# A branch moved into an earlier stage, and identity products in four of TensorE's waits, in a hybrid decoder layer

## The chip, the core and the metric

The kernel runs on one core of one Trainium2 chip. The metric is the device time of one execution in microseconds. The profile names the engines of the core: PE is TensorE's matmul, PEld its weight load, DVE is VectorE, ACT is ScalarE, POOL is GpSimd, and SP is SyncE, whose queue issues most of the transfers.

## The reference

One layer of a decoder for a prompt of 1024 tokens and a sample of 8 sequences with 4 new tokens each, over a paged cache of 8192 positions. A normalised input is projected once and feeds two groups of heads: A, attention over the 256 keys that a small indexer picks for each query, and B, a retention in chunks of 128. All is float32.

```python
h = _rmsnorm(x, g_pre)
qa, ka, va, qi, ki, wi, ga, qb, kb, vb, gb = _project(h, w_in, pos)
# A: indexer, top 256, softmax over the picked keys with a relative bias
s = einsum('bqhd,bsd->bqhs', qi, ki) * D_IDX ** -0.5
score = einsum('bqh,bqhs->bqs', wi, relu(s))        # masked to kpos <= qpos
idx = top_k(score, 256)
oa = softmax(qa . ka[idx] * HEAD_DIM ** -0.5 + rel_bias[bucket]) . va[idx]
# B: per chunk of 128
inter = (qc * dec_in) . S
intra = ((qc . kc) * dmat) . vc
S = S * dec_chunk + (kc * dec_out) . vc
# merge
y = concat(silu(ga) * oa, silu(gb) * head_norm(ob)) . w_out
x = x + _rmsnorm(y, g_post)
x = x + (p . w_ple_up) * sigmoid(x . w_ple_gate)
```

## The kernel before, in words

The kernel is written with a tile framework: the program says which operation an engine does on which tile, a scheduler with a timeline of its own orders each engine's instructions, roughly by their place in the program and by when their operands should be ready, and each engine then works through its queue in that order. What is emitted earlier is preferred. A branch (`tc.If`) divides the program: what stands behind it is put into no queue ahead of what stands before it. `tc.issue_after(x)` keeps the instructions of its block behind `x` in their engine's queue, without a wait.

A float32 product is done either as three products of rounded halves (high and low parts, lines 255 to 257 and 265 to 267), or as one float32 product, which the trace shows as two instructions. PSUM is dealt out in banks of 512 columns through `bank(name, tag)`, with a fixed number of buffers for each tag.

The stages in the order of the program:

1. **First blocks.** Blocks of 128 tokens are loaded, normalised (`norm_x`, line 530 on DVE), transposed on PE and split into high and low parts (`transpose_split`, lines 221, 226 and 227). The norm of three blocks is emitted first; then the first projections follow (`proj_b`), with the rest of the blocks between.
2. **Index scores of the prompt.** For six blocks of 128 queries (`index_scores`, lines 353, 354, 496 and 500). Each block's scores go to `score`.
3. **The sample's index stage.** A loop of 8 sequences by 2 halves, 16 passes. Each pass gathers a piece of the key cache (`kx`, line 797), transposes it on PE (`ptx`, line 807), copies it on ACT (`kT`), multiplies (`pox`, line 811) and applies relu on ACT (`rl`). `later()` emits what was put off: `head_sum` and `by_key`, whose `xe` copies are on DVE (line 786). `unit(1.4)` emits pieces of the projections of `qa`, `ka`, `va` and `ga`. And `tickb` drives the generator `bp`, the prompt's bisection.
4. **The prompt's bisection** (`bisect_prompt`) finds the 256th largest score of each row. It counts (line 659 on DVE, line 655 on ACT for the two longest rows) and fixes one bit per step, then looks at the low half (lines 692 and 694), and takes the eight largest (`top`, line 700). If the tie at the threshold needs more than eight of them, a slow path is taken: `anywhere` sums a flag over the partitions on PE (`pfl`, line 624), DVE reads it (`flp`, line 626) and a branch on DVE (line 709) skips the slow path or not. Behind the branch the masks are made, one block of queries per step (lines 727 to 734).
5. **Retention**, four pairs of heads (`hp`). For each of 8 token blocks PE projects q and k (`pqk`), DVE does the rotary step (`rope`, `rp`, lines 1034 to 1036, finished on POOL); then for each of 8 blocks PE projects v and gate (`pvg`) and `chunk_mm` and what follows do the chunk (lines 1055 to 1065, 1456, 1461 on DVE, 1465, 1467). After the last block `ret_sample` does the sample (lines 1113 to 1135, with `dst` in line 1129). `steps(hp)` is called at each block: it drives the sample's bisection `bss` (`su`, `jv`, `sjk`, `stot`) in the first pair and the sample's selection later, and in the first pair two steps of `bp`. `norm_gate` ends a pair.
6. **Attention of the prompt**, 8 blocks of queries by 2 key heads by 4 heads: scores (`sa`, lines 1563 and 1564), bias and minimum on DVE (line 1569), exponential on ACT (line 1572), transposes (`ptp`, line 1579), products with v (`ob`, line 1587). The sample's attention runs in between.
7. **Merge**: output projection, norm, gate and up projections.

Of the kernel before, what the change touches and what calls it, by code (L numbers as in the profile page):

```python
# [22 lines left out]
NS = 32  # L23
# [97 lines left out]
def tile_step(ctx: ExitStack, tc: tile.TileContext, I, O):  # L121
    nc = tc.nc
# [28 lines left out]

    cst = cp.tile([128, CW], F32, name="cst")

    def C(name, rows=128):
        o, w = _CW[name]
        return cst[:rows, o:o + w]

    ident = C("ident")
# [55 lines left out]
    xl = xp.tile([128, KC, T + NS], F32R, name="xl")  # L214
    xs = xp.tile([128, KC, NS], F32, name="xs")

    def transpose_split(dst_h, dst_l, dst, src, rows):

        pt = pair("pt")
        for c in range(8):  # L220
            nc.tensor.transpose(pt[:, c * rows:(c + 1) * rows], src[:rows, c * 128:(c + 1) * 128],
                                ident[:rows, :rows])
        pt = pt[:, :8 * rows].rearrange("p (j r) -> p j r", j=8)
        for a in range(2):
            ks = slice(a * 4, a * 4 + 4)
            nc.scalar.copy(dst_h(ks), pt[:, ks])
            nc.vector.tensor_tensor(dst_l(ks), pt[:, ks], dst_h(ks).bitcast(F32), op=ALU.subtract)
            if dst is not None:
                nc.vector.tensor_copy(dst[:, ks], pt[:, ks])
# [146 lines left out]
    tickb = [0.0]  # L376
# [89 lines left out]
    with pool("ix", side="right") as ix:  # L466
# [99 lines left out]
            xin[i] = load_x(i)  # L566
        for i in range(3):
            norm_x(i)
        wt.append(load_w("qi1", wcols((QI + 256, 256))))
        nc.sync.dma_start(cst[:, 128:], I["const"][:, 128:CW])  # L570
        todo = list(range(3, 9))
# [221 lines left out]
    for b in range(8):  # L793
        rls = []
        for a in range(2):
            kx = sx.tile([128, 2048], F32, tag="kx", bufs=2, name="kx")
            nc.gpsimd.indirect_dma_start(
                out=kx, out_offset=None, in_=pages,
                in_offset=bass.IndirectOffsetOnAxis(ap=kidx[:, a * 8 + b:a * 8 + b + 1], axis=0))
            for up in range(2):  # L800
                pt = pair("ptx")
                kT = sx.tile([128, 1024], F32, tag="kT", bufs=2, name="kT")
                for u2 in range(2):
                    for i in range(4):
                        r2 = up * 8 + i * 2 + u2
                        c0 = u2 * 512 + i * 128
                        nc.tensor.transpose(pt[:, c0:c0 + 128], kx[:, r2 * 128:(r2 + 1) * 128], ident)
                nc.scalar.copy(kT, pt)
                po = bank("pox", "t")
                for u2 in range(2):  # L810
                    nc.tensor.matmul(po[u2 * 64:u2 * 64 + 64, :], qbd[:, b, :], kT[:, u2 * 512:u2 * 512 + 512],
                                     start=True, stop=True)
                rl = sx.tile([128, 512], F32, tag="rl", bufs=6, name="rl")
                nc.scalar.activation(rl, po, AF.Relu)
                rls.append(rl)
            later()
            tickb[0] += 1.5
            while tickb[0] >= 1:
                tickb[0] -= 1
                step(bp)  # L820
            unit(1.4)
        pend.append(lambda b=b, rls=rls: head_sum(b, rls))
# [219 lines left out]
    def take_vg(src, rows, tb, hp, name):  # L1042
# [6 lines left out]
        nc.scalar.activation(sg[:rows], src[:rows, 128:256], AF.Silu)  # L1049
        return vv.rearrange("p h v -> p (h v)"), sg  # L1050

    def chunk_mm(qk, vv, tb, rows, mask_ap, hp):

        r = bank("ret", "c")
# [7 lines left out]
        sm = rt.tile([128, 2, 128], F32, tag="sm", bufs=2, name="sm")  # L1062
        for j, sc in enumerate((r[:rows, 256:256 + rows], e[:rows, :rows])):
            js = slice(j * 64, j * 64 + 64)
            nc.tensor.matmul(sc, qkT[js, 128:128 + rows], qkT[js, 0:rows], start=True, stop=True)
            nc.vector.tensor_tensor(sm[:rows, j, :rows], sc, mask_ap, op=ALU.mult)
        return r, qkT, sm

# [37 lines left out]
    def ret_sample(hp, qk, sh, acc):  # L1106
# [8 lines left out]
            o = r[NS * (b % 4):NS * (b % 4) + NS, 0:128]  # L1115
            nc.tensor.matmul(o, qm[:, b, :], s0[:, b, :], start=(b < 4), stop=(b >= 4 and b % 4 > 1))
        for j in range(2):
            nc.tensor.matmul(r[NS * j:NS * j + NS, j * 64:j * 64 + 64], sm[:NS, j, :NS], vv[:NS, j * 64:j * 64 + 64],
                             start=False, stop=True)
        nc.scalar.copy(acc[:NS, 8, :], r[NS:2 * NS, 0:128])  # L1120
        for j in (0, 2, 3):
            nc.vector.tensor_tensor(acc[:NS, 8, :], r[NS * j:NS * j + NS, 0:128], acc[:NS, 8, :], op=ALU.add)
# [1 line left out]
        for j in range(2):  # L1124
# [1 line left out]
            vm = rt.tile([NS, 8, 64], F32, tag="vm", bufs=1, name="vm")  # L1126
            nc.vector.tensor_tensor(vm, vv[:NS, None, js].to_broadcast([NS, 8, 64]),
                                    bmask[:, :, None].to_broadcast([NS, 8, 64]), op=ALU.mult)
            nc.tensor.matmul(d[js], qk[:NS, 128 + j * 64:192 + j * 64], vm, start=True, stop=True)
        so = rt.tile([128, 8, 64], F32, tag="vm", bufs=1, name="sso")  # L1130
        for j in range(2):
            js = slice(j * 64, j * 64 + 64)
# [289 lines left out]
    for hp in range(4):  # L1422
# [24 lines left out]
        for tb in range(8):  # L1447
# [10 lines left out]
            for j in range(2):  # L1458
# [3 lines left out]
                else:  # L1462
                    nc.vector.tensor_copy(nxt[js, js], o[js, js])
            if tb:
                nc.tensor.matmul(o, qkT[:, :128], sbd[tb % 2], start=True, stop=False)
            for j in range(2):
                nc.tensor.matmul(o[:, j * 64:j * 64 + 64], sm[:, j, :], vv[:, j * 64:j * 64 + 64],
# [68 lines left out]
    for qb in range(8):  # L1536
# [11 lines left out]
        for kv in range(2):  # L1548
# [5 lines left out]
            for i4 in range(4):  # L1554
                h = 4 * kv + 2 * (i4 % 2) + i4 // 2
                L = (atl, at)[kv].tile([128, T], F32, tag="L", bufs=4, name="L")
                P.append(L)
                mn = ap_.tile([128, 4], F32, tag="mn", bufs=4, name="mn")
                least, i = 3.0e38, 0
                for c in range(0, n, 512):  # L1560
                    wc = min(512, n - c)
                    s = bank("sa")
                    nc.tensor.matmul(s[:, :wc], qas[:, h, :], kah[kv][:, c:c + wc], start=True, stop=False)  # L1563
                    nc.tensor.matmul(s[:, :wc], qas[:, h, :], kal[kv][:, c:c + wc], start=False, stop=True)  # L1564
                    cut = min(max(n - w, c), c + wc)
                    for x0, x1, add in ((c, cut, mask[:, OFF.get(qb, 0) + c:OFF.get(qb, 0) + cut]),
                                        (cut, c + wc, near[:, h - 4 * kv, cut - n + 256:c + wc - n + 256])):
# [243 lines left out]
```

## Time and profile before

| what | value |
|---|---|
| median of 3 runs | 1076.75 us (1073.38 to 1078.46) |
| the profiled execution's own time | 1065.73 us |
| its span, first to last instruction | 1063.9 us |
| mean granted TensorE clock | 0.973 |
| PE busy | 991.7 us, 93% of the span |
| DVE, ACT, POOL busy | 66%, 47%, 27% |
| HBM read and written | 79.25 MB and 21.68 MB |

The page counts for each engine how long it was busy. A row of a timeline reads: start, duration in us, engine, line and operation, what it writes from what, and in square brackets how long the engine was idle before and what ended that wait. A row of the waits reads: who waited for whom, us in total, how often, the longest. The granted clock is 1.00 at full speed of TensorE and 0.50 at half.

### The profile page before, as it was taken

The page shows a single profiled execution, that of the slowest core. Times are in us where ns is not written, and L with a number is a line of the kernel's source. Part 1 is how long each engine was busy: PE and PEld are TensorE (multiplying, and loading weights), DVE is VectorE, ACT ScalarE, POOL GpSimd, SP SyncE. Part 2 cuts the span into 40 slices and gives each one's busy share as a digit, 9 for nine tenths or more (in the row PEclk, how much of TensorE's full clock was granted, in tenths as well). Part 3 has the DMA queues.
Part 4 walks back from the last instruction along what each step waited for, and adds up shares of the span by engine and source line. Part 5 has one row for each costly group of instructions (what it writes and reads, how often), then busy time and mean ns, then how long its engine had stood idle before and what let it go on. Part 6 is the DMA issues. An engine that isn't in the chain of part 4 may idle for free.

```text
span 1063.9 us, 19686 instructions
## 1 busy us (share of the span) xinstructions
PE 991.7 (93%) x7375; PEld 838.6 (79%) x7375; DVE 699.8 (66%) x2012; ACT 504.2 (47%) x1092; POOL 288.1 (27%) x287
## 2 busy tenths in 40 slices
PE   3899998998999789999989995999999999999998
PEld 2899997676776778898788893666656899989998
DVE  6847768999401798978986957887764424874332
ACT  5445554986434356842333435656544523442211
POOL 3102223111201532423632512634340521222100
PEclk8999999999999989999989996899999999999999
DMA  8211235546343311112201425623211312432211
GB/s 291 65 60 51 79 96 169 186 145 202 126 164 111 70 40 41 37 48 87 61 24 41 119 86 149 190 79 105 75 56 47 117 41 80 148 111 82 86 37 40
DMA packets 98308, 102.24 MB, mean 96 GB/s; under 512 B 21346, under 2 KB 88386, under 8 KB 95906
## 3 DMA queue, kind: packets, MB, share of 16 engines
q1 hardware_dynamic: 92450, 74.74, 23.3%
q0 software_dynamic: 5760, 26.22, 7.9%
q8 instruction: 58, 0.95, 0.4%
q14 instruction: 40, 0.33, 0.1%
HBM read 79.25 MB, written 21.68 MB: 95 GB/s over the span
## 4 chain that ended last, share of the span: by engine, by line
PE 53%; DVE 8%; ACT 2%; DMA 2%; issue 1%; POOL 1%; SPq 0%; DVEq 0%; ACTq 0%; POOLq 0%
PE ob L1587 4%; PE ptp L1579 4%; PE pg L265 3%; PE pg L267 3%; PE pg L266 3%; PE po L265 3%; PE po L266 2%; PE po L267 2%; PE pvg L265 2%; PE pvg L266 2%; PE pvg L267 2%; PE sa L1563 2%; PE sa L1564 2%; PE pqk L265 2%; PE pqk L266 1%; PE pqk L267 1%
## 5 line engine op out<-in xcount | busy, mean ns | idle before, releaser
L1147 POOL DMA_INDIRECT kvs<-in_cache_kv,idx x64 | 63.6, 994 | 84.1 <-ACT pT L1584 44.7
L265 PE MATMUL pqk<-whi_qkb,xh 128*128 128x256 f32 x256 | 74.5, 291 | 5.5 <-DVE rp L1036 5.5
L265 PE MATMUL pvg<-whi_vgb,xh 128*128 128x256 f32 x256 | 77.4, 302 | 1.6 <-DVE need L729 1.5
L266 PE MATMUL pvg<-wlo_vgb,xh 128*128 128x256 f32 x256 | 76.6, 299 | 0.0
L267 PE MATMUL pvg<-whi_vgb,xl 128*128 128x256 f32 x256 | 75.2, 294 | 0.0
L266 PE MATMUL pqk<-wlo_qkb,xh 128*128 128x256 f32 x256 | 73.5, 287 | 0.0
L265 PE MATMUL po<-whi_o,yTh 128*128 128x256 f32 x256 | 73.1, 286 | 0.4 <-DVE yaT L1598 0.4
L267 PE MATMUL pqk<-whi_qkb,xl 128*128 128x256 f32 x256 | 73.0, 285 | 0.0
L267 PE MATMUL po<-whi_o,yTl 128*128 128x256 f32 x256 | 72.8, 285 | 0.0
L265 PE MATMUL pg<-whi_g,yTh 128*128 128x256 f32 x256 | 72.7, 284 | 0.0
L266 PE MATMUL po<-wlo_o,yTh 128*128 128x256 f32 x256 | 72.7, 284 | 0.0
L267 PE MATMUL pg<-whi_g,yTl 128*128 128x256 f32 x256 | 72.3, 282 | 0.0
L266 PE MATMUL pg<-wlo_g,yTh 128*128 128x256 f32 x256 | 72.2, 282 | 0.0
L500 DVE SCALAR_TENSOR_TENSOR score<-r,wi,score 128x384 f32<-128x384 f32 (+5 forms) x42 | 44.2, 1053 | 21.0 <-ACT r L496 19.9
L1572 ACT ACTIVATE L<-L,mn 128x128 f32<-128x128 f32 (+7 forms) x64 | 49.5, 775 | 13.7 <-DVE mn L1569 13.6
L265 PEld LDWEIGHTS pqk<-whi_qkb,xh 128*128 128x128 f32 x256 | 48.2, 188 | 9.6 <-issue 6.8
L1768 DVE TENSOR_TENSOR sgm<-pu,sgm 128x256 f32<-128x256 f32 x32 | 13.5, 423 | 61.8 <-PE pu L267 58.6
L265 PEld LDWEIGHTS pvg<-whi_vgb,xh 128*128 128x128 f32 x256 | 50.6, 197 | 3.7 <-issue 1.7
L266 PEld LDWEIGHTS pvg<-wlo_vgb,xh 128*128 128x128 f32 x256 | 50.7, 198 | 0.5
L267 PEld LDWEIGHTS pvg<-whi_vgb,xl 128*128 128x128 f32 x256 | 50.6, 198 | 0.6
L265 PEld LDWEIGHTS po<-whi_o,yTh 128*128 128x128 f32 x256 | 49.0, 191 | 2.2 <-issue 1.6
L496 ACT ACTIVATE r<-si 128x384 f32<-128x384 f32 (+5 forms) x48 | 36.3, 758 | 30.3 <-PE si L354 29.0
(540 smaller groups left out, 3262.1 us busy)
## 6 DMA issues: line engine op xcount, KB each, us to landing
wraw_qkb<-in_w_in SPq DMA_DIRECT2D x16, 256.0 KB
wraw_vgb<-in_w_in SPq DMA_DIRECT2D x16, 256.0 KB
wraw_o<-in_w_out SPq DMA_DIRECT2D x8, 512.0 KB
qas<-qas_d SPq DMA_DIRECT2D x8, 512.0 KB
xr<-in_x_prompt SPq DMA_DIRECT2D x8, 512.0 KB
wraw_g<-in_w_ple_gate SPq DMA_DIRECT2D x8, 512.0 KB
out_y_prompt<-sgm SPq DMA_DIRECT2D x32, 128.0 KB
qas_d<-qst SPq DMA_DIRECT2D x8, 384.0 KB
```

Source lines behind the costliest of these rows:

```text
L265: nc.tensor.matmul(pt[:, :n], ah, hi[:, k, :n], start=(k == 0), stop=False)
L266: nc.tensor.matmul(pt[:, :n], ah, lo[:, k, :n], start=False, stop=False)
L267: nc.tensor.matmul(pt[:, :n], al, hi[:, k, :n], start=False, stop=(k == kc - 1))
L496: nc.scalar.activation(r[:, :n], s[:, :n], AF.Relu)
L500: nc.vector.scalar_tensor_tensor(sc, r[:, :n], wi[:, qb, h:h + 1], sc, op0=ALU.mult, op1=ALU.add)
L1147: return nc.gpsimd.indirect_dma_start(out=dst, out_offset=None, in_=kvflat, in_offset=bass.IndirectOffsetOnAxis(ap=idx, axis=0))
L1563: nc.tensor.matmul(s[:, :wc], qas[:, h, :], kah[kv][:, c:c + wc], start=True, stop=False)
L1564: nc.tensor.matmul(s[:, :wc], qas[:, h, :], kal[kv][:, c:c + wc], start=False, stop=True)
L1572: behind[0] = nc.scalar.activation(L[:, :n], L[:, :n], AF.Exp, bias=least, scale=-1.0, accum_out=sm[:, i4:i4 + 1])
L1579: nc.tensor.transpose(tp[:, i4 * 128:i4 * 128 + 128], P[i4][:, kb * 128:kb * 128 + 128], ident)
L1587: nc.tensor.matmul(ob[64 * o:64 * o + 64, :256], vtok[:, kb, kv * 64:kv * 64 + 64], pT[:, o * 256:o * 256 + 256], start=(kb == 0), stop=(k ...
L1768: nc.vector.tensor_tensor(sg[:rows], usrc, sg[:rows], op=ALU.mult)
```

## The change

It has two parts.

The first is one number. In the sample's index stage `tickb` grows by 2.5 instead of 1.5 per pass, so up to 40 instead of 24 steps of `bp` are emitted in its 16 passes. `bp` has 31 steps.

The second is a helper, `hold(n, behind, tag, w)`: it takes a PSUM bank and emits `n` float32 products of the identity with `w` columns of the table of constants, one behind another, the first of them behind the instruction `behind`. Their result is not read. It is called in four places:

- 40 products of 128 columns behind the last transpose of the second block, ahead of the third block's norm;
- 3 products of 512 columns behind the scores of the last block of the last pair in the retention, ahead of line 1465's product;
- in the last pair's `ret_sample`, 2 and 3 products of 512 columns, one group ahead of each `dst` product;
- 12 products of 512 columns behind the third head's scores in the first block of the attention, ahead of the fourth head's.

```diff
+    def hold(n, behind, tag, w=512):
+        t = bank("hold", tag)
+        for _ in range(n):
+            with tc.issue_after(behind):
+                behind = nc.tensor.matmul(t[:, :w], ident, cst[:, :w], start=True, stop=True).ins
...
         for i in range(3):
             norm_x(i)
+            if i == 1:
+                hold(40, turned[0], "t", 128)
...
             later()
-            tickb[0] += 1.5
+            tickb[0] += 2.5
             while tickb[0] >= 1:
                 tickb[0] -= 1
                 step(bp)
...
+            if hp == 3:
+                hold(2 + j, prior.ins, "b")
+            prior = nc.tensor.matmul(d[js], qk[:NS, 128 + j * 64:192 + j * 64], vm, start=True, stop=True)
...
             if tb:
+                if hp == 3 and tb == 7:
+                    hold(3, score[0], "b")
                 nc.tensor.matmul(o, qkT[:, :128], sbd[tb % 2], start=True, stop=False)
...
                 P.append(L)
+                if qb == 0 and kv == 0 and i4 == 3:
+                    hold(12, scored.ins, "t")
```

The rest of the diff keeps the instructions behind which the products are put: `turned[0]` is the last transpose of a block, `score[0]` the last score product of a chunk, `prior` the product before a `dst`, `scored` the last score product of a head.

More of the change, by code (lines that the diff above doesn't have):

```diff
@@ L215, in tile_step @@
     xs = xp.tile([128, KC, NS], F32, name="xs")
+    turned = [None]
     def transpose_split(dst_h, dst_l, dst, src, rows):
@@ L220, in transpose_split @@
         for c in range(8):
-            nc.tensor.transpose(pt[:, c * rows:(c + 1) * rows], src[:rows, c * 128:(c + 1) * 128],
-                                ident[:rows, :rows])
+            turned[0] = nc.tensor.transpose(pt[:, c * rows:(c + 1) * rows], src[:rows, c * 128:(c + 1) * 128],
+                                            ident[:rows, :rows]).ins
         pt = pt[:, :8 * rows].rearrange("p (j r) -> p j r", j=8)
@@ L1050, in take_vg @@
         return vv.rearrange("p h v -> p (h v)"), sg
+    score = [None]
     def chunk_mm(qk, vv, tb, rows, mask_ap, hp):
@@ L1064, in chunk_mm @@
             js = slice(j * 64, j * 64 + 64)
-            nc.tensor.matmul(sc, qkT[js, 128:128 + rows], qkT[js, 0:rows], start=True, stop=True)
+            score[0] = nc.tensor.matmul(sc, qkT[js, 128:128 + rows], qkT[js, 0:rows], start=True, stop=True).ins
             nc.vector.tensor_tensor(sm[:rows, j, :rows], sc, mask_ap, op=ALU.mult)
@@ L1117, in ret_sample @@
         for j in range(2):
-            nc.tensor.matmul(r[NS * j:NS * j + NS, j * 64:j * 64 + 64], sm[:NS, j, :NS], vv[:NS, j * 64:j * 64 + 64],
-                             start=False, stop=True)
+            prior = nc.tensor.matmul(r[NS * j:NS * j + NS, j * 64:j * 64 + 64], sm[:NS, j, :NS],
+                                     vv[:NS, j * 64:j * 64 + 64], start=False, stop=True)
         nc.scalar.copy(acc[:NS, 8, :], r[NS:2 * NS, 0:128])
@@ L1128, in ret_sample @@
                                     bmask[:, :, None].to_broadcast([NS, 8, 64]), op=ALU.mult)
-            nc.tensor.matmul(d[js], qk[:NS, 128 + j * 64:192 + j * 64], vm, start=True, stop=True)
+            if hp == 3:
+                hold(2 + j, prior.ins, "b")
+            prior = nc.tensor.matmul(d[js], qk[:NS, 128 + j * 64:192 + j * 64], vm, start=True, stop=True)
         so = rt.tile([128, 8, 64], F32, tag="vm", bufs=1, name="sso")
@@ L1563, in tile_step @@
                     nc.tensor.matmul(s[:, :wc], qas[:, h, :], kah[kv][:, c:c + wc], start=True, stop=False)
-                    nc.tensor.matmul(s[:, :wc], qas[:, h, :], kal[kv][:, c:c + wc], start=False, stop=True)
+                    scored = nc.tensor.matmul(s[:, :wc], qas[:, h, :], kal[kv][:, c:c + wc], start=False, stop=True)
                     cut = min(max(n - w, c), c + wc)
```

## The prediction

> **What bounds the kernel now.** I read the page first, then the busy time by stretch of 26.6 us, then TensorE's waits where a stretch is not full, then the VectorE timeline around the prompt's branch.
>
> ```profile
> PE 991.7 (93%) x7375; PEld 838.6 (79%) x7375; DVE 699.8 (66%) x2012; ACT 504.2 (47%) x1092; POOL 288.1 (27%) x287
> ```
>
> TensorE (PE) is busy 93% of the span, so time can come only from its few gaps and from stretches in which its clock is halved. Columns of the next view: stretch, its length, busy us of PE, PEld, DVE, ACT, POOL, then clock, DMA share, GB/s.
>
> ```profile
> 266.00:292.60 26.60, 26.60 (x170) 20.29 (x170) 11.28 (x20) 12.80 (x18) 7.94 (x5) 1.00 0.38 126
> 292.60:319.20 26.60, 26.60 (x159) 19.85 (x158) 0.62 (x4) 9.40 (x14) 1.87 (x2) 1.00 0.50 164
> 319.20:345.80 26.60, 25.64 (x186) 16.93 (x185) 4.18 (x23) 11.81 (x18) 2.80 (x10) 1.00 0.36 111
> 345.80:372.40 26.60, 21.24 (x175) 19.80 (x177) 20.57 (x48) 9.32 (x13) 13.42 (x17) 1.00 0.32 70
> 372.40:399.00 26.60, 22.35 (x159) 20.43 (x148) 26.39 (x62) 13.51 (x31) 8.85 (x10) 0.87 0.15 40
> ```
>
> In the second half of the sample's index stage (266 to 345) PE is full and VectorE (DVE) nearly empty. In the first head pair of the retention (345 to 399) it is the reverse: DVE fills up and PE loses 5.4 + 4.3 us, and the clock falls to a mean of 0.87. What PE waits for from 340 to 480:
>
> ```profile
> PE pqk L265 <- DVE rp L1036: 4.6, 3, 3.0
> PE stot L874 <- DVE sgn L912: 3.2, 2, 2.7
> PE pvg L265 <- DVE need L729: 1.5, 1, 1.5
> PE ret L1055 <- POOL qk L1039: 0.8, 1, 0.8
> ```
>
> All four are DVE results that come late (the POOL one is the rotary step behind DVE). What DVE does there is the prompt's branch and the masks behind it:
>
> ```profile
> 276.64 0.20 DVE L706 TENSOR_REDUCE v<-pick 128x6 f32<-128x48 f32 x1
> 288.09 0.61 DVE L786 COPY xe<-pxt 128x64 f32<-128x64 f32 x4 [11.25 <-PE pxt L782]
> ```
> ```profile
> 344.54 0.14 DVE L626 TENSOR_SCALAR flp<-pfl 1x1 int32<-1x1 f32 x1
> 351.73 0.17 DVE L718 CAST gb<-v 128x6 int32<-128x6 f32 x1 [7.05 <-DVEq L709]
> ```
> ```profile
> L731 DVE TENSOR_TENSOR_SCAN rk<-eq 128x384 f32<-128x384 bf16 (+4 forms) x5 | 8.5, 1703 | 0.0
> L908 DVE TENSOR_SCALAR_CACHE_REDUCE jv<-su,ssm 128x688 bf16<-128x688 uint16 (+1 forms) x8 | 7.4, 922 | 0.0
> L727 DVE TENSOR_SCALAR_CACHE_REDUCE gt<-score,tbits 128x384 bf16<-128x384 f32 (+4 forms) x5 | 4.3, 868 | 0.0
> L928 DVE SCALAR_TENSOR_TENSOR su<-sjk,Xt 128x2080 uint16<-128x2080 uint16 x1 | 3.8, 3774 | 0.0
> L732 DVE SCALAR_TENSOR_TENSOR eq<-rk,need,eq 128x384 bf16<-128x384 f32 (+3 forms) x4 | 3.5, 880 | 0.0
> L730 DVE TENSOR_SCALAR eq<-score,tbits 128x384 bf16<-128x384 f32 (+4 forms) x5 | 2.9, 584 | 0.0
> ```
>
> The search itself has ended at 276.8; then DVE is idle, because the branch is emitted only in the first token block of the retention. There DVE stands still for 7.05 us at the branch, and afterwards lines 727, 730, 731 and 732 alone take 8.5 + 4.3 + 3.5 + 2.9 = 19.2 us by 398, between the rotary steps that PE waits for.
>
> **Part A, the branch moved (`tickb` 1.5 to 2.5).** The generator `bp` has 31 steps. The index loop has 16 passes: at 1.5 it drives 24 steps, up to the last `lw`; the flag (25th), the branch with the first mask (26th) and the other masks come two per block in the retention. At 2.5 the flag comes in the tenth pass, the branch in the eleventh, and all is emitted by the thirteenth. The search runs on DVE at about its own speed either way (it is full until 276.8), so the branch should stand near 280 to 290 and the masks' 19 us and more fall into a DVE that is idle until 340.
>
> Gain: PE's waits above, 4.6 + 3.2 + 1.5 + 0.8 = 10.1 us, of which 9.6 lie before 399 (26.60 - 21.24 and 26.60 - 22.35 in the stretches). Then the clock. Columns: stretch, length, PE busy, clock, DMA share, GB/s:
>
> ```profile
> 12.50:15.80 3.30, 0.26 (x3) 1.00 1.03 417
> 16.00:26.00 10.00, 5.48 (x19) 0.50 0.89 258
> 388.00:394.60 6.60, 6.60 (x28) 0.50 0.00 0
> 394.80:401.40 6.60, 6.60 (x58) 1.00 0.01 2
> 644.00:671.00 27.00, 17.57 (x79) 0.50 0.42 116
> ```
>
> Right behind the longest wait for `stot` (2.7 us) the clock is 0.50 for 6.6 us, in which PE issues 28 products against 58 in the next 6.6: half, so about 3.3 us. Without the wait there is no halving; gain 12.9 us in all. Against it: (1) the sample's own bisection goes on, a chain over DVE, ScalarE (ACT) and PE; some wait for `stot` stays: +2.0, between 0 and the 3.2 of its row. (2) Nothing behind the branch can be put ahead of it in a queue, so at its new place the last `pox` waits for its own `kT` copy: +1.3, between nothing and the longest such wait, 4.8, nearest to the ACT copy of about 1.0 below. (3) The search is emitted earlier, so its counts are preferred to the unit's copies of the same pass: +1.5 (bounds under the rivals). (4) The 7.05 us standstill moves along but holds up only `xe` copies, which the timeline shows 11 us apart and more, and units of the last kind (`ga`), that ACT alone takes: 0, or up to 7 if an `xe` falls into it. SP's and POOL's queues get no new step; the masks issue no DMA. Sum of A: -12.9 + 4.8 = -8.1 us.
>
> [...]
>
> **Part B, 40 products behind the second block's transposes.**
>
> ```profile
> 8.80 1.97 PE L221 MATMUL pt<-cst,x 128*128 128x128 f32 x8 [8.80 <-DVE x L530]
> 10.97 1.79 PE L221 MATMUL pt<-cst,x 128*128 128x128 f32 x8 [0.19 <-DVE rv_x L234]
> 19.63 1.94 PE L221 MATMUL pt<-cst,score 128*128 128x128 f32 x8 [6.88 <-DVE xl L227]
> 22.46 0.57 PE L255 MATMUL pb<-xh,wkih 128*72 128x384 f32 x1 [0.89 <-ACT xh L226]
> ```
> ```profile
> 37.49 0.30 PE L221 MATMUL pt<-cst,mask 128*128 128x128 f32 x1 [2.92 <-DVE rv_x L234]
> ```
> ```profile
> 630.28 0.22 PE ret L1456 x2
> ```
>
> A float32 product of 128 columns is two instructions, 0.22 us at full clock. 40 x 0.22 = 8.8 us in a gap of 6.88: the third block's transposes start at 12.76 + 8.8 = 21.6 instead of 19.63, but at full clock (half of 1.94), so the first projection starts about 1 us late and then runs 3.5 us of half-clock work in half the time. PE is thus about 0.7 us early at 26, yet then waits for DVE at 37.49 anyway, and DVE gets the third block's transposes 2 us late. From -0.5 to +2 at full clock; I take +1.0. At half clock throughout the 40 take 17.6 us, 10.7 more than the gap: the far end.
>
> **Part C, the retention's end.** 3 products ahead of the last block's L1465, 2 and 3 ahead of the two `dst`, 12 ahead of the fourth head's scores, all of 512 columns.
>
> ```profile
> PE sa L1563 <- DVE mn L1569: 7.9, 1, 7.9
> PE ret L1465 <- DVE sbd L1461: 1.9, 1, 1.9
> PE dst L1129 <- DVE vm L1127: 1.2, 2, 0.8
> ```
> ```profile
> 437.53 1.00 PE dst L1129 x2
> ```
> ```profile
> 643.90:646.60 2.70, 2.70 (x26) 0.50 1.15 306
> ```
>
> 512 columns are four times 0.22, so 0.87 us each at full clock (`dst`, of that width, takes 1.00 with its latency). Against the gaps: 3 x 0.87 - 1.9 = +0.7; 5 x 0.87 - 1.2 = +3.1. These stand on the chain (DVE `sbd`, PE L1465, `dst`, DVE `sso`, norm). Given back at full clock: two `dst` from about 2 to 1 us each (-2.0), and L1465, L1467, L1116 in front of them (-1.4, half of 2.7 us at clock 0.50). 12 x 0.87 = 10.4 against 7.9: +2.5, of which the table load and the first three exponentials on ACT hide all but about 0.5. Then full clock from 661 to 671, 10 us that ACT shares with PE: -3, between 0 and -5. Sum: +0.7 + 3.1 - 3.4 + 0.5 - 3 = -2.1; from -5 to +4 (the eight products in front at half clock cost another 7 us, less what full clock brings earlier).
>
> **Sum.** -8.1 + 1.0 - 2.1 = -9.2 us. The profiled execution took 1065.7 us (span 1063.9), 1.0% under the median of the runs, 1076.75; the stages are the same, so I take the difference over: 1067.5 us.
>
> **Rivals.**
> (i) The waits come back elsewhere. With DVE relieved, the sample's bisection becomes the late one (its L908 and L928 rows above already take 11.2 us of the same stretch), PE waits for `stot` instead of `rp`: A shrinks to about -3, the total to -4: 1073. For it: the `stot` wait is the second longest. Against it: DVE's order had put the scan L731 between the counts.
> (ii) Slower: the search crowds out the copies that feed PE. ACT from 186 to 240:
>
> ```profile
> L655 ACT ACTIVATE js<-mask,cand 128x896 bf16<-128x896 bf16 (+1 forms) x23 | 25.6, 1113 | 4.2 <-DVE cand L680 4.0
> L808 ACT COPY kT<-ptx 128x1024 f32<-128x1024 f32 x12 | 12.2, 1025 | 0.0
> L814 ACT ACTIVATE rl<-pox 128x512 f32<-128x512 f32 x10 | 6.2, 624 | 0.5 <-PE pox L811 0.3
> ```
>
> If each of the 12 `kT` and 10 `rl` copies waits for one more `js`, that is 22 x 1.1 = 24 us; if PE's second buffer hides a quarter, 18 us: 1067.5 + 18 - 1.5 = 1084. It decides from ten such waits on, 11 us, which take all of the gain. Against it: the steps are emitted at about the rate at which DVE finishes them, so few are ahead.
> (iii) The products run at half clock themselves. The half-clock stretch from 16 to 26 lasted on through the first 3.5 us of dense products (from 22.46), so the clock rises only behind some dense work. If it is low when B starts and rises 7 us on, 16 products at 0.44 and 24 at 0.22 take 12.3 us, 5.4 over the gap; with C at its end of +4 the total is -8.1 + 5.4 + 4 = +1.3, or 1078. [...] In this trace the transposes at 8.80 took 1.97 us, as at half clock, and the clock row from 12.5 on reads 1.00: it rose just as B would start, which suits B.
>
> **How the numbers follow.** Forecast as summed, B and C near nothing: 0.55. Rival (i): 0.20. (ii): 0.10. (iii): 0.15. Half a per cent, 5.4 us, is about what tells a change from none here. Faster by more than that: the forecast and a little of (i), 0.61; within: most of (i) and half of (iii), 0.25; slower: (ii) and some of (iii), 0.14. The likeliest case's own range is 1060 to 1072 (A from -12.9 + 1.5 to -4, C from -5 to +1); over the cases 1058 to 1079.
>
> **What will show it.** A right: `flp` near 280 to 290, the masks done by 330, PE full from 345 to 399, no halved clock near 388. A wrong: PE idle again for `stot`, or waits of PE for `kT` and `rl` that grow between 186 and 266. B right: clock 1.00 from 12.5 on and the first projection before 24; wrong: the stop at 37.49 moved back by more than 2 us. C right: clock 1.00 from 641 to 671, `dst` at 1.00; wrong: halved while the products run, or `sso` later than its place relative to L1465 before. Most damaging would be (ii), as PE is full from 266 to 345 and has nothing there to absorb it with.

## The result, and the profile after

The changed kernel took 1082.75 us (median of 22 runs, 1076.29 to 1086.42) against 1076.26 us before (22 runs on the same chips, 1071.0 to 1079.81): a ratio of 1.0059, 95% interval 1.0044 to 1.0075, some 6.4 us slower. The prediction was 1067.5 us, 1058 to 1079.

The traces need one caution. The execution of before from which the prediction was made has a span of 1063.9 us. Two more traces of the same kernel have 1074.4 and 1070.9. The one after has 1082.2. So of the 18 us between the first pair of traces some 12 are chance, as the medians differ by 6.4. Below, "before" in a comparison of stages is the trace with 1074.4 where nothing else is said.

The page of the changed kernel, its first line of busy times:

```profile
PE 1016.2 (94%) x7495; PEld 856.6 (79%) x7495; DVE 704.6 (65%) x2012; ACT 502.5 (46%) x1088; POOL 286.4 (26%) x287
```

PE is 24.5 us busier than in the line of the prediction, and the span is 18.3 us longer. The `hold` products alone run for 28.6 us (the rows of L158 below). They were to fill 17.9 us of waits, but all of PE's waits together, the span less its busy time, fell only from 72.2 us (75.4 in the second trace) to 66.0. The lengths of the stages in us, each from the first product of one tile to the first of the next (`si`, `ptx`, the first `pqk` of each pair, `sa`, `po`, `pg`, end):

| trace | first blocks | prompt scores | index stage | pair 1 | pair 2 | pair 3 | pair 4 | attention | `po` | rest | span |
|---|---|---|---|---|---|---|---|---|---|---|---|
| before, the prediction's | 54.6 | 125.5 | 159.5 | 72.3 | 69.4 | 81.2 | 89.3 | 173.6 | 108.9 | 129.5 | 1063.9 |
| before, second | 56.1 | 125.4 | 160.5 | 72.4 | 69.4 | 81.9 | 89.5 | 179.4 | 108.8 | 130.9 | 1074.4 |
| before, third | 56.8 | 125.5 | 163.0 | 70.5 | 69.1 | 80.9 | 89.6 | 173.6 | 109.9 | 132.0 | 1070.9 |
| after | 63.1 | 125.6 | 162.7 | 64.1 | 76.6 | 81.2 | 91.5 | 177.4 | 108.5 | 131.5 | 1082.2 |

Three things stand out: the first blocks are 7 us longer, pair 1 is 8 us shorter as forecast, and pair 2 is 7 us longer.

**First blocks.** PE's timeline after:

```profile
13.84 9.26 PE L158 MATMUL hold<-cst 128*128 128x128 f32 x80
22.94 1.04 PE L229 MATMUL pt<-cst,score 128*128 128x128 f32 x8
...
28.54 0.57 PE L263 MATMUL pb<-xh,wkih 128*72 128x384 f32 x1 [2.39 <-ACT xh L234]
...
34.65 0.59 PE L264 MATMUL pb<-xl,wkih 128*72 128x384 f32 x1 [5.22 <-DVE xl L235]
```

The products ran at full clock (9.26 us for 40), and the transposes behind them too (1.04 us, half of 1.94). But PE then waited 2.4 us for `xh` and 5.2 us for `xl` of the third block; before, it waited 0.9 us for that `xh` and not at all for the `xl`. What DVE and ACT did meanwhile, and POOL beside them (one fence for each engine's timeline):

```profile
27.15 2.32 DVE L323 CAST lf<-pti 128x8 f32<-128x8 int32 x1
29.39 2.38 DVE L326 TENSOR_SCALAR kf<-ptf,cst 128x8 f32<-128x8 f32 x1
...
33.91 2.03 DVE L235 TENSOR_TENSOR xl<-pt,xh 128x512 fp32r<-128x512 f32 x3
```
```profile
27.82 1.07 ACT L234 CAST xh<-pt 128x512 fp32r<-128x512 f32 x2
```
```profile
26.26 5.48 POOL L186 TENSOR_TENSOR wlo_qi<-wraw_qi,whi_qi 128x1024 fp32r<-128x1024 f32 x2 [2.71 <-ACT whi_qi L185]
```

The third block's `xl` stands at 33.91 behind the norms of later blocks and the page table's little instructions. In the kernel before (first trace), DVE did its second half at 24.32:

```profile
24.32 0.67 DVE L227 TENSOR_TENSOR xl<-pt,xh 128x512 fp32r<-128x512 f32 x1
```

The reading is that the scheduler counts the 9 us of products, expects the third block's transposes late, and gives the queues of DVE and ACT other work first; a run below tests it. Two of those small instructions took 2.32 and 2.38 us instead of 0.16 and 0.22 (first trace of before) while POOL was in its two products: they end at 29.47 and 31.77, POOL's products at 29.44 and 31.74.

**Retention.** Stretches as in the prediction (PE, PEld, DVE, ACT, POOL busy, clock, DMA share, GB/s), after:

```profile
319.20:345.80 26.60, 26.60 (x166) 18.69 (x165) 13.75 (x25) 11.62 (x18) 2.08 (x5) 1.00 0.39 130
345.80:372.40 26.60, 23.22 (x187) 19.08 (x185) 8.87 (x26) 8.23 (x11) 11.79 (x15) 1.00 0.46 112
372.40:399.00 26.60, 24.56 (x188) 23.13 (x188) 19.59 (x62) 17.08 (x38) 11.06 (x19) 0.87 0.15 41
```
```profile
302.19 0.17 DVE L728 CAST gb<-v 128x6 int32<-128x6 f32 x1 [1.37 <-DVEq L719]
```
```profile
472.20 0.22 DVE L991 SCALAR_TENSOR_TENSOR ssm<-ssm 128x1 f32<-128x1 f32 x1 [3.20 <-DVEq L975]
```

The branch is at 300.7 to 302.2, some 10 us behind the forecast's 280 to 290, and the masks are out of the retention's way. DVE stands still for 1.37 us there, not 7.05. But the second branch, the sample's, now costs 3.20 us where it cost 0.90 or 0.91 in the three traces of before. And PE is not full from 345 to 399: it waits 3.4 + 2.0 us there instead of 5.4 + 4.3, and the clock's mean from 372 to 399 is 0.87 as before, halved from 372.6 to 379.4 around a wait of 3.1 us for `rp`.

**Retention's end and attention.** PE's timeline after, then the same place in the prediction's trace of before:

```profile
648.19 0.49 PE L1481 MATMUL ret<-sbd,qkT 128*128 128x128 f32 x2 [0.57 <-DVE sbd L1475]
...
649.87 2.84 PE L158 MATMUL hold<-cst 128*128 128x512 f32 x6
...
654.86 0.49 PE L1481 MATMUL ret<-sbd,qkT 128*128 128x128 f32 x2 [1.30 <-DVE sbd L1475]
...
656.89 3.17 PE L158 MATMUL hold<-cst 128*128 128x512 f32 x4
659.98 1.07 PE L1143 MATMUL dst<-vm,qk 32*64 32x512 f32 x2
660.98 2.84 PE L158 MATMUL hold<-cst 128*128 128x512 f32 x6
663.75 1.07 PE L1143 MATMUL dst<-vm,qk 32*64 32x512 f32 x2
664.75 0.33 PE L1581 MATMUL sa<-kahi,qas 128*128 128x128 f32 x1
...
665.47 10.51 PE L158 MATMUL hold<-cst 128*128 128x512 f32 x24
675.42 0.62 PE L1581 MATMUL sa<-kahi,qas 128*128 128x128 f32 x1
...
678.16 0.65 PE L1605 MATMUL ob<-pT,vtok 128*64 128x256 f32 x4 [0.68 <-ACT pT L1602]
```
```profile
639.16 0.49 PE L1465 MATMUL ret<-sbd,qkT 128*128 128x128 f32 x2 [0.57 <-DVE sbd L1461]
...
643.88 0.79 PE L1465 MATMUL ret<-sbd,qkT 128*128 128x128 f32 x2 [1.93 <-DVE sbd L1461]
...
651.86 0.47 PE L1563 MATMUL sa<-kahi,qas 128*128 128x128 f32 x1
...
661.29 0.48 PE L1563 MATMUL sa<-kahi,qas 128*128 128x128 f32 x1 [7.89 <-DVE mn L1569]
...
667.36 1.12 PE L1587 MATMUL ob<-pT,vtok 128*64 128x256 f32 x4
```

From the seventh block's product to the first score: 16.6 us after, 12.7 before. From there to the fourth head's score: 10.7 against 9.4. From there to the first `ob`: 2.7 against 6.1, at full clock. In sum +1.8 us.

### The profile page after: what moved, and what is told of

It reads as the page before. It is cut to its first block, busy times and chain, and to the rows that moved or that the text cites. A ratio compares the mean times of both kernels' runs of the same rounds, so it can differ in the third digit from the quotient of the medians.

```text
span 1082.2 us, 19931 instructions
## 1 busy us (share of the span) xinstructions
PE 1016.2 (94%) x7495; PEld 856.6 (79%) x7495; DVE 704.6 (65%) x2012; ACT 502.5 (46%) x1088; POOL 286.4 (26%) x287
## 4 chain that ended last, share of the span: by engine, by line
PE 43%; DVE 6%; DMA 3%; issue 2%; ACT 1%; POOL 1%; SPq 1%; ACTq 0%; DVEq 0%; POOLq 0%
PE ob L1605 4%; PE ptp L1597 3%; PE po L273 3%; PE po L275 3%; PE po L274 3%; PE pg L273 2%; PE pg L275 2%; PE pg L274 2%; PE sa L1581 2%; PE pvg L273 2%; PE hold L158 1%; PE sa L1582 1%; PE pvg L274 1%; PE pvg L275 1%; DMA out_y_prompt<-sgm 1%
## 5 line engine op out<-in xcount | busy, mean ns | idle before, releaser
L273 PE MATMUL pg<-whi_g,yTh 128*128 128x256 f32 x256 | 72.9, 285 | 1.5 <-ACT sgm L1785 1.5
L273 PE MATMUL po<-whi_o,yTh 128*128 128x256 f32 x256 | 73.1, 286 | 0.2 <-ACT yTh L1647 0.2
L275 PE MATMUL pg<-whi_g,yTl 128*128 128x256 f32 x256 | 72.3, 283 | 0.0
L274 PE MATMUL pg<-wlo_g,yTh 128*128 128x256 f32 x256 | 72.2, 282 | 0.0
L275 PEld LDWEIGHTS pqk<-whi_qkb,xl 128*128 128x128 f32 x256 | 50.1, 196 | 2.5 <-issue 2.4
L273 PEld LDWEIGHTS pg<-whi_g,yTh 128*128 128x128 f32 x256 | 48.8, 190 | 3.5 <-ACT sgm L1785 1.9
L1785 ACT ACTIVATE sgm<-pg 128x256 f32<-128x256 f32 x32 | 12.3, 386 | 84.2 <-PE pg L275 69.9
```

The lines of the kernel that those rows point to most:

```text
L273: nc.tensor.matmul(pt[:, :n], ah, hi[:, k, :n], start=(k == 0), stop=False)
L274: nc.tensor.matmul(pt[:, :n], ah, lo[:, k, :n], start=False, stop=False)
L275: nc.tensor.matmul(pt[:, :n], al, hi[:, k, :n], start=False, stop=(k == kc - 1))
L1785: nc.scalar.activation(sg[:rows], gsrc, AF.Sigmoid)
```

## The experiments

All times are against 17 to 29 runs of the kernel before on the same chip; each run of the table stands for 6 to 12 executions, and the ratio has its 95% interval.

| run | what it holds | ratio | first `si` | pair 1 | pair 2 |
|---|---|---|---|---|---|
| `e1_branch` | A | 0.9990 (0.9968 to 1.0012) | 56.2 | 67.4 | 76.5 |
| `e2_first` | B | 1.0118 (1.0081 to 1.0155) | 64.1 | 73.7 | 68.7 |
| `e3_end` | C | 1.0026 (1.0000 to 1.0053) | 56.3 | 73.3 | 68.6 |
| `e4_branch_end` | A and C | 1.0029 (1.0007 to 1.0051) | 57.0 | 65.2 | 78.2 |
| `e6_first_prio` | B, third block early | 1.0174 (1.0143 to 1.0206) | 61.6 | 73.7 | 68.6 |
| `e7_first_12` | B with 12 products | 1.0004 (0.9978 to 1.0030) | 54.1 | 70.5 | 69.1 |
| `e8_early_nosif` | A, no sample branch | 0.9988 (0.9966 to 1.0011) | 55.9 | 65.4 | 74.3 |
| `e9_late_nosif` | before, no sample branch | 1.0031 (1.0010 to 1.0053) | 56.4 | 72.9 | 68.8 |
| `e10_nomask` | before, masks nearly free | 1.0016 (0.9994 to 1.0037) | 56.0 | 64.1 | 76.6 |
| `e11_first_28` | B with 28 products | 1.0082 (1.0057 to 1.0108) | 56.1 | 72.9 | 68.7 |
| `e12_end_12` | C's 12 products | 1.0004 (0.9983 to 1.0026) | 56.3 | 70.4 | 69.1 |
| `e14_first_28b` | B with 28, again | 1.0060 (1.0039 to 1.0082) | 56.2 | 73.1 | 68.7 |
| `e15_end_8` | C's 8 products | 1.0033 (1.0014 to 1.0052) | 56.3 | 74.4 | 68.9 |
| `e16_twelves` | A, 12 first, C's 12 | 1.0019 (0.9996 to 1.0043) | 55.2 | 66.9 | 76.5 |
| `e17_first_order` | B, two orders added | 1.0068 (1.0045 to 1.0091) | 56.7 | 73.2 | 68.7 |
| `e18_after_order` | whole change, two orders added | 1.0027 (1.0006 to 1.0048) | 55.7 | 64.2 | 76.9 |

### The parts alone

Each of the four takes lines out of the changed kernel: the `hold` calls that it lacks, and `+= 2.5` goes back to `+= 1.5` where A is not in it. B alone, for instance:

```diff
-            tickb[0] += 2.5
+            tickb[0] += 1.5
...
-            if hp == 3:
-                hold(2 + j, prior.ins, "b")
...
-                if hp == 3 and tb == 7:
-                    hold(3, score[0], "b")
...
-                if qb == 0 and kv == 0 and i4 == 3:
-                    hold(12, scored.ins, "t")
```

> Only part A (the bisection generator driven by 2.5 steps per pass, so that the branch falls inside the sample's index stage); no extra products. Theory 1 (the branch is worth what the sum said, the products are what cost): the first head pair of the retention shrinks from 72.4 to about 64 us, first blocks unchanged, and the whole is 5 to 8 us faster than before: about 1069 us, ratio 0.992 to 0.996. Rival 1 (the waits return: the index stage grew by 3 us and the second head pair by 7 us in the changed kernel, and both belong to the branch): first pair 64, second pair 76, index stage +3, whole within 2 us of before, ratio 0.998 to 1.002.

> Only part B (40 products of 128 columns behind the second block's transposes); 1.5 steps per pass, no products at the retention's end. Theory 1: the first blocks end 8 us later, as in the changed kernel (first si product at 63 instead of 54.6), and nothing gives it back: +7 to +9 us against before, ratio 1.006 to 1.009. Rival 1 (the 8 us of the first blocks are swallowed by later waits, as PE has 70 us of them): within 3 us of before.

> Only part C (3, 2, 3 and 12 products of 512 columns at the retention's end and the attention's beginning). Theory 1: products take 17 us of TensorE of which the waits cover 11, the clock stays up and returns about as much: -1 to +3 us against before, ratio 0.999 to 1.003. Rival 2 (the products push back the first scores and with them the attention's chain: the stage from the first scores to the end grew by 4 to 6 us in the changed kernel): +4 to +6 us, ratio 1.004 to 1.006. Prediction's own figure: -2.1 us.

> Parts A and C without B (no products at the first blocks). Theory 1: the first blocks as before (first si product at about 54.6), first head pair 64 us, whole 6 to 8 us faster than the changed kernel and 1 to 7 us faster than before: 1069 to 1075 us. Rival 1 (waits come back in the second head pair and index stage): about 1076 to 1079, the gain against the changed kernel still 8 us of the first blocks less what is swallowed.

A alone is 1.1 us faster, an interval from 3.4 faster to 1.3 slower: rival 1 was right, the waits return; with C it is worth nothing either (1.0029 against 1.0026), so the fourth run fell on the rival's side too, and at 1080.75 us even above its 1076 to 1079. B alone is 12.7 us slower, more than either theory had, 8 of it in the first blocks. C alone is 2.8 us slower, as Theory 1 had it. The parts do not add up: -1.1, +12.7 and +2.8 make 14.4, the whole change measured 6.4. On top of A and C, B costs only about 3 us (1.0059 against 1.0029, whose intervals overlap a little).

### Where A's gain goes

First the sample's branch, where DVE stood for 3.2 us and PE waited 1.9 us for `sbits`:

```diff
-        with tc.If(many > 0):
-            c4 = cg[:NS, :4]
...
         V.scalar_tensor_tensor(v, v, sg, c65, op0=ALU.mult, op1=ALU.add)
```

> Part A alone, and the sample's branch with its sixteen-pass fallback left out. Theory (part A's 7 us of the first head pair are lost at the sample's branch in the second: TensorE waits 1.9 us for sbits and 0.7 for second, VectorE stands 3.2 us where it stood 0.9 before, and no work emitted behind the branch can fill): second head pair about 70 us instead of 76.5, the whole 4 to 7 us faster than part A alone: ratio to before 0.992 to 0.996. Rival (TensorE's work and clock set the pace and the waits move on to the next block): second pair shorter, later ones longer, ratio 0.997 to 1.001.

> The kernel before with the sample's branch and its fallback left out: the control for the run of part A without that branch. Theory (in the kernel before VectorE stands there 0.9 us only and TensorE does not wait): within 2 us of before, ratio 0.998 to 1.002. Rival (the branch as a border in the queues costs something whatever part A does): as much faster as the early one, ratio 0.993 to 0.997.

Without the branch A has the same time (0.9988 against 0.9990). The theory falls. Without it the kernel before is 0.3% slower, so a branch less is not by itself a gain.

Then the bound: what could the whole of this DVE work be worth? The next kernel leaves out the prompt's branch with its slow path and the ranking of ties, so it no longer computes the layer exactly; it only shows the time without that work.

```diff
-        with tc.If(many > 0):
...
         for j, o, n in lens:
-            jj = slice(j, j + 1)
...
-            V.tensor_scalar(mask[:, o:o + n], gt[:, :n], -BIG, BIG, op0=ALU.mult, op1=ALU.add)
+            V.tensor_scalar(mask[:, o:o + n], score[:, o:o + n], tf[:, j:j + 1], BIG, op0=ALU.is_le, op1=ALU.mult)
             yield
```

> The kernel before with the prompt's branch and its fallback left out, and each prompt mask made by one threshold comparison, without the ranking of ties (one VectorE instruction per block instead of seven: about 24 us less VectorE work in the first head pair, and no 7 us standstill). Part A can do no more for the retention than take this work out of it. Theory 2 (what VectorE saves in the first head pair, TensorE loses again where VectorE or the sample's chain is the limit in later pairs): first pair 64 to 66 us, second 75 to 78, whole within 3 us of before, ratio 0.997 to 1.002. Rival (part A's gain is real and only its new place in the index stage costs it): 6 to 9 us faster, ratio 0.991 to 0.995.

Nothing: 1.0016. Theory 2 was right. Pairs 1, 2 and 4 by stretches (edges are the pairs' first `pqk` products and the first `sa`), second trace of before, then A alone, then this run:

```profile
342.10:414.50 72.40, 63.94 (x489) 58.90 (x488) 63.02 (x161) 31.22 (x65) 23.35 (x29) 0.93 0.22 55
414.50:483.90 69.40, 68.93 (x571) 61.56 (x572) 56.55 (x207) 44.01 (x105) 23.02 (x37) 1.00 0.18 48
...
565.80:655.30 89.50, 85.48 (x719) 72.51 (x718) 64.74 (x277) 33.96 (x97) 30.21 (x39) 0.95 0.40 108
```
```profile
344.80:412.20 67.40, 60.33 (x486) 56.80 (x485) 38.12 (x126) 35.42 (x75) 22.21 (x31) 0.95 0.25 58
412.20:488.70 76.50, 73.85 (x592) 64.90 (x590) 60.97 (x215) 40.61 (x99) 26.27 (x39) 1.00 0.21 56
...
568.70:657.60 88.90, 81.48 (x683) 69.54 (x682) 64.20 (x258) 30.14 (x90) 29.13 (x39) 0.94 0.40 108
```
```profile
341.60:405.70 64.10, 57.74 (x492) 54.20 (x494) 38.28 (x127) 35.48 (x75) 22.07 (x31) 1.00 0.25 61
405.70:482.30 76.60, 73.81 (x595) 64.89 (x594) 60.86 (x215) 40.56 (x98) 26.21 (x39) 1.00 0.21 56
```

DVE has 25 us less to do in pair 1 (63.0 to 38.1), and the pair is 5 to 8 us shorter. In pair 2 PE issues 592 products instead of 571, and with 2 us of new waits the pair is 7 us longer. In pair 4 it issues 683 instead of 719, 4 us less work, and the pair is as long as before: its waits grow from 4.0 to 7.4 us. So part of the chunks' work stands earlier in PE's queue (by tiles, first trace of before against A alone: `ret` and `second` products 136 to 156 in pair 2, 214 to 188 in pair 4), and in the last pair, which it had filled, PE now waits instead. New or longer waits of A alone, in pair 2 (first line) and in pair 4 (the other two; before has 1.2 us for `dst` there and none for `psl`):

```profile
PE ret L1466 <- DVE sbits L991: 1.9, 1, 1.9
PE dst L1139 <- DVE vm L1137: 2.8, 2, 2.0
PE psl L1258 <- DVE lo__5444 L1266: 1.6, 1, 1.6
```

In pair 1 itself the waits did not go with the masks either. This is PE's longest one with the masks left out:

```profile
PE pqk L265 <- DVE rp L1015: 4.2, 2, 3.1
```

It is 2.6 to 4.6 us in the three traces of before and 3.8 with A alone. The run shows that relief in pair 1 is worth nothing (within 0.4%) in either of the two ways that were tried. That the last pair is set by these chains of small results, and not by one engine, is read from the traces alone; no run took them apart.

### What B costs

> Part B alone, its 40 products kept, but the third block's norm and splits are emitted at high priority, so that its xl splits stand in VectorE's queue behind 15 instructions fewer and its xh copies ahead of the weight casts. Theory (the order of VectorE's queue is what part B costs: xl came at 33.9 us instead of 22.6, behind the norms of later blocks): the first si product comes at 57 to 59 instead of 64.1, and the whole is 5 to 7 us faster than part B alone (1090.5): ratio to before 1.004 to 1.007. Rival (the 9.3 us of the products themselves are the cost): si at 62 to 64, ratio 1.010 to 1.013.

> Part B alone with 12 products instead of 40 (2.6 us at full clock, inside the old wait of 6.9), with which the third block's xl splits stand at VectorE rows 34 and 42 against 33 and 37 without any and 57 with 40. Theory (queue order): about as before, si within 2 us of 56, ratio 0.999 to 1.004. Rival (products at the head cost whatever their number, as the clock's phase or the PSUM bank is at fault): ratio above 1.007.

The first changes one line pair, the second the count:

```diff
         for i in range(3):
-            norm_x(i)
+            if i == 2:
+                with tc.high_priority():
+                    norm_x(i)
+            else:
+                norm_x(i)
```
```diff
-                hold(40, turned[0], "t", 128)
+                hold(12, turned[0], "t", 128)
```

Twelve products cost nothing that can be told (within 0.3%). The first blocks even end 2 us earlier than in the second and third trace of before, but that is not seen in the time. The high priority gave the worst time of all, and is no clean answer: when three tenths of the `pb` products are done, PE is level with the kernel before (97.2 us against 98.0; B alone 106.1), but the order changed further on as well, and at the start of the index stage PE waits 9.0 us for a gathered page of keys. So next only the two places were changed (`split` keeps the last `xh` copy and the last `xl` split), and the count once more:

```diff
+        third = list(split)
+        with tc.issue_after(third[0]):
+            wt.append(load_w("qi1", wcols((QI + 256, 256))))
...
+        with tc.issue_after(third[1]):
+            load_pt()
```

> Part B alone with all its 40 products, and two orders of issue added: on VectorE the page table's work (the lines from ptf to base) is queued behind the third block's xl splits, on ScalarE the casts of the second qi weights behind its xh copies. Nothing else is moved. Theory (what the 40 products cost is that these two are queued ahead: xh at 27.8 and xl at 33.6 us instead of 23.6 and 24.6): the first si product at 57 to 60 instead of 64.1, the whole 4 to 7 us faster than part B alone (1090.5), ratio to before 1.004 to 1.008. Rival (the products' own 9.3 us): si at 62 to 64, ratio 1.010 to 1.013.

> Part B alone with 28 products: 6.1 us, which fit into the old wait of 6.7 us, so that they move no transpose; but the third block's xl splits stand at VectorE rows 49 and 55 (33 and 37 without products, 34 and 42 with 12, 57 with 40). Theory (the place in VectorE's and ScalarE's queues costs): first si product at 60 to 63, ratio 1.004 to 1.009. Rival (only what goes past the wait costs): si at 54 to 56 as with 12, ratio 0.998 to 1.002.

> The 28 products once more. Its trace showed the first si product at 56.1, as without products, and yet the kernel was 8.8 us slower than before by its runs. If that is real, the ratio comes out at 1.006 to 1.011 again and the trace shows a later stage that is longer by 3 us and more than in the kernel before; if it was the runs' scatter, 0.999 to 1.004.

PE and DVE in `e17_first_order`:

```profile
13.57 10.34 PE L158 MATMUL hold<-cst 128*128 128x128 f32 x80
...
29.00 0.40 PE L265 MATMUL pb<-xl,wkih 128*72 128x384 f32 x1 [2.77 <-DVE xl L236]
```
```profile
28.26 2.03 DVE L236 TENSOR_TENSOR xl<-pt,xh 128x512 fp32r<-128x512 f32 x3
```

All 40 products are there, `xl` comes at 28.26 instead of 33.6, the first `si` at 56.7 instead of 64.1, and about 5 us of the 12.7 are gone. So the delay of the first blocks was the queues' order, not the products' 9 us. With 28 products the splits stand early enough and the first blocks are not late either (56.1 and 56.2), which the theory had wrong.

But 28 products measured 8.8 and 6.4 us slower, and 40 with the order mended 7.3, and up to the third pair their traces show no delay against the second trace of before (within 2 us). Where these 7 us lie is open. One guess was more time at half clock: counted from 100 us on, the five traces of B with 28 or 40 products have 59 to 76 us of it (the expectation below, which has 62 to 79, counted a little past the last instruction). The third trace of before was made to see whether that is unusual:

> The kernel before once more, for a second trace, as its profiled execution was 10 us shorter than its median. If that execution was only lucky in the page gathers (TensorE did not wait for kvs in it), the stage from the first scores to the output projection takes 178 to 183 us here instead of 173.6, and the first si product comes at 56 instead of 54.6; the retention's four pairs come out within 2 us of 72.3, 69.4, 81.2 and 89.3.

> The kernel before a third time, for the trace: how much of the time behind 100 us runs at half clock. If the kernels with 28 and 40 products (62 to 79 us in five traces) differ from it by more than the scatter, it shows 50 to 61 us as the kernels without them did; if not, it may show 62 or more. The stage from the first scores to the output projection between 173 and 183 us.

The third has 65.4, the second 59.4, the first 48.0: single traces scatter too far to decide. The mean granted clock, which is on record for every run, decides more. Span times (1 - mean clock), an estimate of the most that the halved clock can have cost, is longer than in the runs of before on the same chip in all five kernels: by 5.0 and 2.3 us with 28 products, by 3.4, 3.9 and 1.9 with 40 (`e2_first`, `e6_first_prio`, `e17_first_order`). With 12 it is the same (-0.2). Two of the five, `e11_first_28` and `e6_first_prio`, stand clear of the scatter. So more time at half clock is probably part of these 7 us; where it comes from, and where the rest lies, stays open. The stage up to `po` is 179.4 us in the second trace and 173.6 in the third: it scatters by 6 us in the kernel before.

### C by halves, and the rest

One run has of C only the calls `hold(3, ...)` and `hold(2 + j, ...)`, the next only `hold(12, ...)`; neither has A or B.

> Of part C only the 3, 2 and 3 products at the last block and the two dst. Theory (they lengthen the chain at the retention's end and give back nothing, since the clock falls behind them): fourth head pair 92 to 95 us instead of 89, ratio 1.002 to 1.006. Rival (they pay for themselves by full clock, as predicted): ratio 0.997 to 1.001.

> Of part C only the 12 products ahead of the fourth head's scores. Theory (the 8 products on the chain at the retention's end are what part C costs, 6 us of the fourth head pair, and the 12 give back about 3 to 4 at full clock): fourth pair 89 as before, scores to output projection 177 to 179 instead of 178 to 183, whole 1 to 4 us faster than before, ratio 0.996 to 0.999. Rival (the 12 alone do not hold the clock, since it falls before them): ratio 0.999 to 1.003.

The 8 products cost 3.5 us, the 12 nothing that can be told (+0.4), where their theory had 1 to 4 us of gain: they give back what they take. With the 8 alone pair 4 is 96.3 us instead of 89.5; the last `sbd` is still waited for (2.52 us against 1.93), so they did not fill that wait but moved it. Some of it may have come back: the stage up to `po` took 171.1 us in that trace, below the 173.6 to 179.4 of before.

The last two start from the changed kernel. One has 12 for 40 in B and none of C's 8; the other keeps all and adds the two orders shown above:

```diff
-                hold(40, turned[0], "t", 128)
+                hold(12, turned[0], "t", 128)
...
-            if hp == 3:
-                hold(2 + j, prior.ins, "b")
...
-                if hp == 3 and tb == 7:
-                    hold(3, score[0], "b")
```

> Part A, 12 products at the first blocks and the 12 of the attention's beginning, none of the 8 at the retention's end: the parts that cost nothing alone. If they add up, 0.995 to 0.999 of before (2 us of the first blocks, 1 of the branch, 0 to 2 of the attention); if each gain is lost later, 0.999 to 1.002.

> The whole change (A, B with 40 products, C), with the two orders of issue added: the page table's VectorE work behind the third block's xl splits, the second qi weights' ScalarE casts behind its xh copies. Theory (B's cost is mostly these two places): the first si product at 56 to 58 instead of 63.1, 4 to 6 us faster than the whole change, ratio to before 1.000 to 1.003. Rival (the products cost what they cost, wherever the splits stand): ratio 1.004 to 1.008, as the whole change.

The harmless parts together gain nothing. With the order mended the whole change loses half of its loss (1.0059 to 1.0027), as far as A and C stand without B. So the loss of the whole change is accounted for: A is worth nothing, C costs about 3 us, which is what its 8 products cost alone, and B's 3 us on top are the order of the queues, as far as intervals of some 2 us each can tell. What stays open is B alone, which still costs 7 us with the order mended. No version is measurably faster than the kernel before.

## Why the prediction was wrong, point by point

**A, forecast -8.1, measured -1.1 (-3.4 to +1.3).** The step that failed is the gain itself, 9.6 us of waits and 3.3 of clock counted as time. That there is no halving without the wait was the author's inference from one place: with the masks left out the clock is 1.00 all through pair 1, with one wait of 3.1 us for `rp` in it; in the changed kernel, with a wait as long, it is halved for 6.8 us. The place was nearly right (branch 10 us late, PE full to 345), and pair 1 lost 6 to 8 us in the whole change, 3 to 5 with A alone. But its two halves failed. The waits were put down to the masks, and most of them stayed: PE's waits in pair 1 are 7.1 us with A alone and 6.4 with the masks left out, against 8.3 to 9.6, and the one for `rp` is as long as before. And a wait that vanishes is only time if what follows is bound by the same engine, and here what pair 1 won came back in pairs 2 and 4, as work that stands earlier and as waits for small results. That was rival (i), at 0.20, in size (A at -3 lies within the interval) but not in its mechanism: the wait for `stot` in pair 1 fell, from 2.7 us and more to 1.5, and the new waits are for several other results. Taking the masks out altogether shows the same. The terms against it were small as forecast: the last `kT` wait was there with and without the change (4.9 and 5.0 us), so the +1.3 for the branch as a border was not needed; the index stage takes 159.4 to 163.3 us with A and 159.0 to 163.4 without it. Rival (ii) did not come: no new waits for `kT` or `rl`. The standstill did not "move along" whole: it came again at the new place, but with 1.37 us instead of 7.05, and the sample's branch then took 3.2 instead of 0.90. No run shows what sets these lengths.

**B, forecast +1.0, measured +12.7 alone and about +3 on top of A and C.** The products' own time was right (0.23 us each, full clock, transposes at 22.9), so rival (iii) did not come. What failed is "DVE gets the third block's transposes 2 us late": the order of the queues was taken as fixed, though the scheduler makes it anew with the products in its timeline. The sign named for this, the stop at 37.49 moved back by more than 2 us, came in a worse form: 7.6 us of waits ahead of 28.5 and 34.7, where 0.9 had been. Mending that order gave back about 5 of the 12.7 us; the other 7 stay open, as said above. The premise on the clock was weak too. In the prediction's trace the clock rose at 12.4 and fell again; in nine of the ten other traces with the old first blocks it rose first at 26.4 to 29.3. With the products in place it rose at 12.4 to 16.2 in all nine traces; none shows the 7 us that rival (iii) lets pass before it rises, and so this rival cost at most the 1.2 us by which the 40 products took longer in `e6_first_prio` and `e17_first_order` (10.3 us) than in `e2_first` (9.1).

**C, forecast -2.1 with -5 to +4, measured +2.8 (0 to +5.7).** Given back at full clock: -3.3 behind the 12 products (forecast -3), the `dst` at about half their time as forecast (0.61 us an instruction against 1.08). The 12 in place of the 7.9 us wait: +1.2 (forecast +0.5). Two terms were mis-sized. The 3 products (forecast +0.7, as they fill 1.9 us of waiting) were issued ahead of the sample's chunk products, and PE still waited 1.30 us for `sbd`: from one L1481 to the next 6.67 us instead of 4.72, +1.95. Behind that wait the clock fell, with the next two products running at half of it:

```profile
655.90:659.30 3.40, 3.40 (x23) 1.61 (x16) 2.15 (x10) 1.90 (x4) 0.00 (x0) 0.50 0.34 80
```

So the five products took 3.1 + 2.8 us in place of 1.2 us of waits, +4.7 instead of +3.1, and the products in front of them gave back 0.9 instead of 1.4. In this trace these terms make +1.8 us, where -2.1 was forecast.

**The base.** The forecast took the traced execution, 1% under the median, as the same stages at the same ratio. Two more traces show the stage from the first scores to `po` at 173.6 and 179.4 us in the same kernel.

## What to carry to other kernels

A wait of the busiest engine is worth its length only if the stages behind it are bound by that engine too; leave the late work out altogether once, and see what the whole kernel gains, before moving it. Filler on an engine's queue is also filler in the scheduler's timeline: look at where the other engines' next instructions land, above all what stands ahead of the operand that the filler was to bridge. Take two or three traces of the kernel before, when the gain looked for is 1%.

## What the runs showed of the hardware that was not expected

- DVE stood still for 5.5 to 8.3 us at the prompt's branch in its old place (13 traces), and in the new one for 1.4 us (five traces) and 3.65 (`e18_after_order`). At the sample's branch, which was not moved, it stood for 0.90 us where the prompt's branch was in its old place (12 traces), and for 3.2 to 3.5 where that was moved (five) or left out (`e10_nomask`).
- Two instructions on 8 columns on DVE took 2.32 and 2.38 us instead of 0.16 and 0.22 while POOL was in 128x1024 products, and each ended within 0.03 us of one of them. It was so in the kernel before too: one on a single column took 2.34 us in the first trace and ended at 27.99, POOL's product at 27.97. No run shows what joins the two.
- At the start of a trace the clock column did not tell the clock. In the first trace of before it says 1.00 ahead of 12.4 us, while the transposes at 8.80, 1.04 us at full clock in the changed kernel (those at 22.94), took 1.97. The durations of a known product tell it.
- Between 600 and 700 us the clock is halved for 27 us in all three traces of before, for 17 with the 12 products alone, and for 3 to 10 with all 20 of C. The time of the kernel did not follow. Over all runs of C alone the mean granted clock rose from 0.969 to 0.979, by the estimate above worth at most 11 us, and the kernel was 2.8 us slower: the products, and what they pushed back, took more than the clock gave.
